# New order tables for VectorE, ScalarE, GpSimd and the transfer queue of a hybrid decoder layer

## The chip, the cores and the metric

The kernel runs on one core of a Trainium2 chip. A core has five instruction streams: TensorE (matmuls; PE in the rows, and PEld for its weight loads), VectorE (DVE), ScalarE (ACT), GpSimd (POOL) and SyncE (SP), which issues the transfers between memory and the core. Each engine works through its own instructions in the order in which they were written, and waits where an input is not there yet or a buffer is still in use. The metric is the time of one launch in microseconds on the device.

## The reference

One decoder layer on x of 512 positions by 1024 features, all in float32:

- h = RMSNorm(x), then one projection h @ w_in, whose columns are split among three groups of heads;
- gated DeltaNet, 4 heads of 128: a causal convolution of width 4 and SiLU on q, k and v, a decay and a beta per head from the gate columns, the delta rule in chunks of 64 (the inverse of a triangular matrix, then a state passed from chunk to chunk), a gated RMSNorm;
- S5, 32 groups of 16 channels: a diagonal complex state of 64 per group scanned over the positions, GELU, a gated linear unit (w_glu), RMSNorm;
- differential attention, 4 heads, two causal softmax maps per head subtracted with a learned factor, RMSNorm;
- x = x + concat(groups) @ w_out;
- x = x + (silu(gate) * up) @ w_down, where gate and up are a causal convolution of width 3 over RMSNorm(x) @ w_up (2 x 2816 columns); then a final RMSNorm.

The reference does these lines in this order:

```
g_q, g_k, g_v, g_z, g_b, g_a, s_u, d_q, d_k, d_v = split_cols(h @ w_in[i], IN_SIZES)
qkv = jax.nn.silu(causal_dwconv(jnp.concatenate([g_q, g_k, g_v], axis=-1), gdn_conv_w[i]))
x = x + jnp.concatenate([o_gdn, o_s5, o_diff], axis=-1) @ w_out[i]
x = x + conv_glu_ffn(rms_norm(x, ffn_norm_w[i]), ffn_w_up[i], ffn_conv_w[i], ffn_conv_b[i], ffn_w_down[i])
return rms_norm(x, final_norm_w)
```

## The kernel before

Every float32 product with a weight is done in three matmuls: the weight block (128 x 512, 256 KB, "wraw") is cast by ScalarE into a rounded high part ("whi", L566), VectorE subtracts it from the raw block for the low part ("wlo", L263), and TensorE adds high x high, low x high and high x low of weights and activations into one accumulator ("acc", helper at L182; transposes are the same instruction at L185). A block has three buffers, so its transfer (L564, on SyncE) starts when the block three before it has been used up. `wblock` (L555 to 568) does this for all weights.

The mixers take the first 465 us. Their generators run side by side: the projections (L1401 to 1426), the gates and decays of DeltaNet (gates L896 to 907 with the tile gg, decays L910 to 955), the convolutions `conv_silu` (L963 to 970: a product, three shifted multiply-adds into kq on VectorE, the sigmoid thc on ScalarE, a product), the DeltaNet chain (L1078 to 1225: scr and ms/rs are the norms of q and k, sc and lt the scaled triangular matrix, lct, xc, t_ and f_ the steps of its inverse), S5 (its scan L662, its outputs yu, which go out to memory and come back in another layout as yf: one write L694, four reads L696), and the differential heads (dv and dqk are copies of projections, L1252 and L1268; ka, kl, qa their split parts; pp the softmax). After that comes the output projection, and from 530 us the feed-forward network.

TensorE's order is a table of items (`ORDER`, L37), written out by hand and by a planner. When all is written, `in_order` (L135) pins the order of the four other engines: `SEQUENCE` (L55 to 129) has one list of numbers per engine, and the k-th number says which of the engine's instructions, counted as the program wrote them, stands at place k. SyncE's list is the order of the transfers in its queue; each issue there also waits for the landing of the one eight before it.

Of the kernel before, what the change touches and what calls it, by code (L numbers as in the profile page):

```python
# [78 lines left out]
784 779 787 782 790 785 794 788 774 791 777 793 780 783 800 786 789 792 801 795 802 1121-1122 796-799 1123 810 1124
803 1125-1126 804 806 811 815 805 807 816 808 1127-1128 812 821-822 813 809 814 817 826 818-819 827 823 832 820  # L80
824-825 833 828 837 829-830 838 831 834 843 835-836 844 839 848 840-841 849 842 845 854 846-847 855 850 859 851-852
860 853 856 865 857 867 858 869 861 866 871 862 868 873 863 870 875 872 874 877 879 864 876 881 878 882 880 886-887
883 892 884-885 893 888 897 889-890 898 891 894 903 895-896 904 899 908 900-901 909 902 905 914 906-907 915 910 919
911-912 920 913 916 925 917-918 927 921 929 922-923 926 931 924 928 933 930 935 932 937 934 939 936 941 938 942 940
946-947 943 952 944-945 953 948 957 949-950 958 951 954 963 955-956 964 959 968 960-961 969 962 965 974 966-967 975
970 979 971-972 980 973 976 985 977-978 987 981 989 982-983 986 991 984 988 993 990 995 992 997 994 999 996 1001 998
1002 1000 1006-1007 1003 1012 1004-1005 1013 1008 1017 1009-1010 1018 1011 1014 1023 1015-1016 1024 1019 1028
1020-1021 1029 1022 1025 1034 1026-1027 1035 1030 1039 1031-1032 1040 1033 1036 1045 1037-1038 1047 1041 1049
1042-1043 1046 1051 1044 1048 1053 1050 1055 1052 1057 1054 1059 1056 1061 1058 1062 1060 1066-1067 1063 1072
1064-1065 1073 1068 1077 1069-1070 1078 1071 1074 1083 1075-1076 1084 1079 1088 1080-1081 1089 1082 1085 1094  # L90
# [4 lines left out]
0-1 3 2 5 4 6-24 27 25 29 33 26 28 51 30 44 31 46 34-35 43 52 45 36 39 49 37 40 38 41-42 57 32 50 53 55-56 92 97
58-59 54 62-64 60 65-66 61 67 69-76 68 77-81 86-87 82-85 108 93-94 88-89 102-104 47 95 110 105-106 90 48 91 107 96
121 123 109 98 111-114 99-101 115-117 124-125 122 118 126 150-151 131-132 127-128 146 137-139 129 119 140 144 130
141 120 142 147 145 148-149 133-136 168 143 174 152-154 158 156 189 159 190-191 155 192 157 160-161 164 166 165 162
186 169 167 170-173 197-202 175 212 163 176 214 178 177 179 183 185 180 184 187 181 193-194 188 195-196 204-207 203
215 208-211 182 222-223 220 213 257 216 259 217 225 221 218 256 258 226 228 224 229 232 227 219 233 236 230 237 231  # L100
234 253 235 238-241 246-247 242-245 248-249 252 254 262 250-251 268 255 271 260-261 265 263-264 266-267 275 283 269
274 270 286 272-273 278-281 276-277 289 282 297-298 293-294 292 284 295-296 285 308 287-288 319 290-291 299-301 329
305 302 306 303 332 334 304 312 307 311 313 309-310 314 331 333 315-316 352 317 353 318 344 320 354-355 321-322 326
323 327 347 330 335 324-325 336-337 342 328 356-357 343 361 338-341 362-364 358 345 359 348 365-368 349 393 346 396
360 350-351 370-373 378 374-377 386 379 384-385 387 380-381 388 369 391 408 389-390 392 382 394-395 383 404 406 399
415 397-398 403 405 400-401 419 402 407 409-410 420 411-414 416 426 417 427 418 421-425 429 432 461-462 457-460 443
428 430-431 446 435 433-434 436-437 452 440-441 438-439 444-445 453 442 489 491 449 488 490 447 455 450 448 456 451
454 475 463 476 464-465 469 467 466 484 470 468 471 473 494 474 495-496 477 497 472 478-479 485 480-481 533 482-483
486-487 492 498 493 509-512 499-501 534 502 513-516 508 503 537 518-525 504-507 532 538 526-529 517 535 546 536
530-531 552 539-540 566 543-544 541-542 547-548 545 567 551 553-556 549-550 557-558 561 559-560 562-563 586-587  # L110
564-565 576 582-583 568 584 569 585 577 570-573 579 574-575 580-581 578 598 603 588-590 594 592 591 595 593 596-597
607 599-601 617 602 604-606 618 608-612 620 613-616 623 619 626 629 622 621 632 625 635 624 628 627 638 631 630 641
634 633 644 637 636 645 640 639 646 643 642 647 869-872 653 873 648 874-875 649 876 654 656 650 657 651 661 652 662
655 664 659 658 665 669 660 663 670 667 672 666 673 668 677 671 678 675 680 674 681 676 685 679 686 683 688 682 689
# [6 lines left out]
""",  # L121
    "gpsimd": """
0 4 1 10 3 5 7 6 57-60 9 8 11-12 61-62 13-19 21 26 20 22 27 30 33 36 39 28 31 34 37 40 29 32 35 38 41 45 42 46 43 47
44 48 66-67 23 50 25 49 54 51 53 52 56 55 68-69 63-65 70 73 75 72 74 71 78 80 77 79 76 81-83 85 87 86 84 88 90 92 89
91 94 93 95-130
""",
    "sync": """
# [1712 lines left out]
```

## Time and profile before

| | us |
|---|---|
| median of 3 runs | 829.7 (827.82 to 830.31) |
| the profiled execution | 831.47 |
| its span, first to last instruction | 829.3 |
| TensorE busy in the span | 792.8 |
| VectorE busy | 561.9 |
| ScalarE busy | 430.8 |
| GpSimd busy | 104.4 |

The mean granted clock of TensorE over the span is 0.972. The span is what the profiler saw of one execution; the 2.2 us between it and the execution's own time lie around the first and the last instruction. A share of busy time is a mean over stages: in the feed-forward part TensorE is busy all the time, in the mixers it waits here and there.

### The profile page before, as it was taken

Reading aid. Unit: us, or ns where it says so; the run is one execution under the profiler, and the core shown is the slowest. Engines: PE = TensorE matmul, PEld = TensorE weight load, DVE = VectorE, ACT = ScalarE, POOL = GpSimd, SP = SyncE. Lnnn points to the kernel's source line nnn. Section 1 sums busy time; section 2 is a strip of 40 time slices with the busy share of each in tenths; the row PEclk is TensorE's granted clock in tenths of the full one; section 3 lists DMA queues with packets and bytes.
Section 4 is the critical chain, followed back from the end, with each engine's and each line's share of the span. In section 5 each row is a group of like instructions: output and inputs, shape, how many; then the busy total and the mean of one; then the engine's idle time right before and its main releaser. Section 6 shows DMA issues by size and latency. Waiting matters only on the chain.

```text
span 829.3 us, 13695 instructions
## 1 busy us (share of the span) xinstructions
PE 792.8 (96%) x5004; PEld 653.9 (79%) x5004; DVE 561.9 (68%) x1159; ACT 430.8 (52%) x1001; POOL 104.4 (13%) x133
## 2 busy tenths in 40 slices
PE   6979989998999999999999999999999999999996
PEld 6868877986777878787777788788888888888885
DVE  8998898754757866548447976766557656657634
ACT  5266356644567966675547644344244334335423
POOL 5710000000001210010003211011001001001101
PEclk8998999998998999999989999999999999999998
DMA  6856453378383633341214532333333333333202
GB/s 158 102 94 51 92 77 87 61 111 61 81 45 53 44 67 72 94 70 55 84 44 125 182 100 83 107 102 90 101 90 101 102 89 102 95 96 100 78 1 102
DMA packets 133562, 71.58 MB, mean 86 GB/s; under 512 B 12766, under 2 KB 129784, under 8 KB 133496
## 3 DMA queue, kind: packets, MB, share of 16 engines
q1 hardware_dynamic: 133496, 70.72, 40.6%
q8 instruction: 39, 0.64, 0.3%
q14 instruction: 27, 0.22, 0.1%
HBM read 66.51 MB, written 4.19 MB: 85 GB/s over the span
## 4 chain that ended last, share of the span: by engine, by line
PE 74%; DVE 11%; DMA 6%; ACT 4%; issue 2%; POOL 1%; SPq 1%; POOLq 0%; DVEq 0%; ACTq 0%
PE acc L182 62%; PE gp L182 5%; PE sp L182 4%; DMA wraw<-in_w_in_dram 4%; DVE wlo L263 2%; DVE kq L269 1%; PE sp L185 1%; DVE z L263 1%; PE gp L185 1%; DMA yf<-swap 1%; ACT whi L566 1%; DVE ct L263 1%; DVE z L662 1%; ACT gm L1022 1%; DVE zt L263 0%
## 5 line engine op out<-in xcount | busy, mean ns | idle before, releaser
L566 ACT CAST whi<-wraw 128x512 fp32r<-128x512 f32 (+2 forms) x224 | 133.2, 597 | 169.1 <-PE acc L182 142.5
L182 PE MATMUL acc<-h,whi 128*128 128x512 f32 x704 | 217.7, 390 | 0.0
L263 DVE TENSOR_TENSOR wlo<-wraw,whi 128x512 fp32r<-128x512 f32 (+2 forms) x224 | 151.7, 680 | 55.7 <-ACT whi L566 49.9
L182 PE MATMUL acc<-hT,whi 128*128 128x512 f32 (+1 forms) x464 | 154.2, 409 | 4.7 <-ACT dv L1252 2.9
L182 PEld LDWEIGHTS acc<-h,whi 128*128 128x128 f32 x704 | 132.1, 188 | 28.6 <-DVE h L269 0.6
L182 PE MATMUL acc<-h,wlo 128*128 128x512 f32 x352 | 137.0, 390 | 0.0
L182 PEld LDWEIGHTS acc<-hT,whi 128*128 128x128 f32 x464 | 88.6, 198 | 20.6 <-ACT dv L1252 3.1
L182 PE MATMUL acc<-hT,wlo 128*128 128x512 f32 (+1 forms) x240 | 92.6, 398 | 0.0
L263 DVE TENSOR_TENSOR x<-x,acc 128x512 f32<-128x512 f32 (+1 forms) x65 | 44.0, 677 | 57.3 <-PE acc L182 57.3
L182 PEld LDWEIGHTS acc<-h,wlo 128*128 128x128 f32 x352 | 66.1, 188 | 14.0 <-DVE wlo L263 0.3
L269 DVE SCALAR_TENSOR_TENSOR ac<-us,rt,ac 128x511 f32<-128x511 f32 x88 | 65.9, 750 | 12.9 <-ACT ac L1719 11.5
L263 POOL TENSOR_TENSOR ac<-ac 128x512 f32<-128x512 f32 x22 | 35.6, 1619 | 280.5 <-DVE ac L269 161.3
L182 PE MATMUL acc<-ah,whi 128*128 128x512 f32 x144 | 57.6, 400 | 0.1
L182 PE MATMUL acc<-ah,wlo 128*128 128x512 f32 x144 | 56.5, 392 | 0.0
L182 PE MATMUL acc<-al,whi 128*128 128x512 f32 x144 | 56.0, 389 | 0.0
L401 POOL TENSOR_TENSOR rs<-ms,expo 128x4 f32<-128x4 f32 (+1 forms) x14 | 19.3, 1375 | 278.8 <-DVE ms L400 274.6
L182 PEld LDWEIGHTS acc<-hT,wlo 128*128 128x128 f32 x240 | 46.4, 198 | 7.5
L263 DVE TENSOR_TENSOR us<-acc,rb 128x512 f32<-128x512 f32 x44 | 30.3, 688 | 27.9 <-PE acc L182 27.9
L1719 ACT ACTIVATE ac<-us,rt 128x512 f32<-128x512 f32 x44 | 36.0, 817 | 21.5 <-DVE us L263 21.5
L263 DVE TENSOR_TENSOR al<-ac,ah 128x512 fp32r<-128x512 f32 x22 | 15.2, 691 | 28.1 <-ACT ah L1733 27.5
L182 PEld LDWEIGHTS acc<-ah,whi 128*128 128x128 f32 x144 | 27.1, 188 | 6.7 <-issue 1.1
L1733 ACT CAST ah<-ac 128x512 fp32r<-128x512 f32 x22 | 13.7, 622 | 35.8 <-POOL ac L263 35.8
(567 smaller groups left out, 1404.2 us busy)
## 6 DMA issues: line engine op xcount, KB each, us to landing
wraw<-in_ffn_w_up_dram SPq DMA_DIRECT2D x88, 256.0 KB
wraw<-in_w_in_dram SPq DMA_DIRECT2D x64, 256.0 KB
wraw<-in_ffn_w_down_dram SPq DMA_DIRECT2D x32, 256.0 KB
wraw<-in_w_out_dram SPq DMA_DIRECT2D x24, 128.0 KB
xt<-in_x_dram SPq DMA_DIRECT2D x4, 512.0 KB
xj<-in_x_dram SPq DMA_DIRECT2D x8, 256.0 KB
wraw<-in_w_out_dram SPq DMA_DIRECT2D x8, 256.0 KB
lwraw<-in_ffn_w_down_dram SPq DMA_DIRECT2D x8, 256.0 KB
```

Of the source, the lines that this page charges most:

```text
L182: pe(T.matmul(o, l, r, start=start, stop=stop))
L185: pe(T.transpose(o, i, ident_))
L263: e.tensor_tensor(o, a, b, op=op)
L269: e.scalar_tensor_tensor(o, a, s, b, op0=op0, op1=op1, **kw)
L401: ins = G.tensor_tensor(rs[:, :n], ms[:, :n], expo[:, :n], op=ALU.pow)
L566: S.copy(hi[:, :n], raw[:, :n])
L662: V.tensor_tensor_scan(zf[j], rr, zf[j], 0.0, ALU.mult, ALU.add)
L1022: S.activation(gm[:, n, :], m_ge, AF.Copy, scale=gp[:, n, h : h + 1])
L1719: S.activation(a, us, AF.Identity, scale=fcw(2, f), bias=fcb(f))
L1733: S.copy(ah[:, j, :], up)
```

## The change

Only the four lists of `SEQUENCE` differ: the lists for VectorE, ScalarE, GpSimd and SyncE are new. No instruction is added or taken away, TensorE's table is untouched, and the arithmetic is the same. Nearly all moves are in the first 465 us; a few lie between 463 and 530 us, and the last is a swap of two VectorE instructions at the very end. A list looks like this, so its numbers tell a reader nothing:

```diff
-98-102 114-117 107 118 108 119 109-111 120-123 128-195 200-219 223 348-351 224 352-355 225-347 356-363
+114-118 107 119-120 108-111 121-123 128-195 200-219 223 348-350 224 351-355 225-347 356-363
```

What it does is seen in the engines' orders, the old one with -, the new one with +.

First place: VectorE just ahead of the gate tile gg. gt is a chain of small steps towards it, z and zt are rotations of the S5 input, wlo is the low part of a weight block.

```order
 L263 TENSOR_TENSOR z<-sp,cs 128x512
 L269 SCALAR_TENSOR_TENSOR gt<-gt,gs 128x16
-L263 TENSOR_TENSOR cs<-cs,ct 128x512
+L263 TENSOR_TENSOR zt<-sp,cs 128x512
 L263 TENSOR_TENSOR gt<-gt,gmx 128x16
-L263 TENSOR_TENSOR z<-sp,cs 128x512
+L269 SCALAR_TENSOR_TENSOR zt<-sp,cs 128x512
 L269 SCALAR_TENSOR_TENSOR gg<-gt,al 128x16
-L263 TENSOR_TENSOR zt<-sp,cs 128x512
+L263 TENSOR_TENSOR wlo<-wraw,whi 128x512
 L944 CAST ghi<-gg 128x16
```

Both zt products now stand ahead of gg; a wlo that came after it has also moved ahead, further up than the piece shows.

Second place: ScalarE around the copy dv (the values of a differential head, out of the accumulator that TensorE fills next). ff are copies of the inverse's last step f__1437, d and enx parts of S5's tables.

```order
 L742 COPY wt<-sp 128x512 x2
-L1160 COPY ff<-f__1437 32x4x32
+L1160 COPY ff<-f__1437 32x4x32 x3
+L790 COPY enx<-en 64x32x16
 L773 COPY d_120<-sp 128x4x32
-L775 COPY d_120<-sp 32x4x32 x2
 L1252 COPY dv_1458<-acc 128x512
-L790 COPY enx<-en 64x32x16
-L775 COPY d_120<-sp 32x4x32
+L775 COPY d_120<-sp 32x4x32 x3
+L776 COPY d_120<-sp 64x4x32
```

Two more ff copies and an enx have moved ahead of dv, two d copies behind it.

Third place: VectorE and ScalarE where the second pair of heads has its keys and queries convolved (kq), about 190 to 210 us. VectorE before, from the first shifted step of the last kq on:

```order
L269 SCALAR_TENSOR_TENSOR kq<-acc,rt,kq 128x511
L269 SCALAR_TENSOR_TENSOR kq<-acc,rt,kq 128x510
L263 TENSOR_TENSOR wlo<-wraw,whi 128x512
L269 SCALAR_TENSOR_TENSOR kq<-acc,rt,kq 128x509
L269 SCALAR_TENSOR_TENSOR kq<-thc,kq 128x512
L400 TENSOR_SCALAR ms<-ss 128x8
L263 TENSOR_TENSOR wlo<-wraw,whi 128x512
L263 TENSOR_TENSOR sc<-rs,beta 128x4
```

And now:

```order
L269 SCALAR_TENSOR_TENSOR kq<-acc,rt,kq 128x511
L269 SCALAR_TENSOR_TENSOR kq<-acc,rt,kq 128x510
L269 SCALAR_TENSOR_TENSOR kq<-acc,rt,kq 128x509
L269 SCALAR_TENSOR_TENSOR kq<-thc,kq 128x512
L263 TENSOR_TENSOR wlo<-wraw,whi 128x512
L400 TENSOR_SCALAR ms<-ss 128x8
L263 TENSOR_TENSOR sc<-rs,beta 128x4
```

The wlo that stood between the second and the third step stands behind the whole kq, and the next wlo has moved from ahead of sc to behind lt. ScalarE in the same place, before (scr are the squares for the norms, kt the scaled keys):

```order
L963 ACTIVATE kq<-acc,rt 128x512
L566 CAST whi<-wraw 128x512
L968 ACTIVATE thc<-kq 128x512
L1078 ACTIVATE scr,ss<-gp 128x128 x4
L1081 ACTIVATE kt<-gp,ed 128x128 x2
L1078 ACTIVATE scr,ss<-gp 128x128 x4
L1081 ACTIVATE kt<-gp,ed 128x128 x2
L1268 ACTIVATE dqk<-acc 128x512
L566 CAST whi<-wraw 128x512 x2
L1115 COPY lct<-lt 32x128 x2
```

And now:

```order
L963 ACTIVATE kq<-acc,rt 128x512
L968 ACTIVATE thc<-kq 128x512
L566 CAST whi<-wraw 128x512
L1078 ACTIVATE scr,ss<-gp 128x128 x8
L1081 ACTIVATE kt<-gp,ed 128x128 x3
L1268 ACTIVATE dqk<-acc 128x512
L1081 ACTIVATE kt<-gp,ed 128x128
L1115 COPY lct<-lt 32x128
L566 CAST whi<-wraw 128x512
L1115 COPY lct<-lt 32x128
L566 CAST whi<-wraw 128x512
```

The cast of the same weight block has moved behind thc, and the cast of the block after it behind the first lct.

## Rows read from the trace of the kernel before

**Rows 1.** the page, part 1: busy us (share) xinstructions of each engine.
```profile
PE 792.8 (96%) x5004; PEld 653.9 (79%) x5004; DVE 561.9 (68%) x1159; ACT 430.8 (52%) x1001; POOL 104.4 (13%) x133
```

**Rows 2.** the chain that ended last: start us, us, what.
```profile
529.77 250.13 PE acc L182 x1098
```

**Rows 3.** timeline of TensorE: start us, us, what [idle before <- what ended it].
```profile
60.78 0.36 PE L182 MATMUL gp<-gg,m_ge 128*128 128x16 f32 x2 [3.36 <-DVE gg L269]
...
113.70 0.99 PE L182 MATMUL acc<-hT,whi 128*128 128x512 f32 x2 [2.94 <-ACT dv L1252]
...
138.62 0.60 PE L182 MATMUL sp<-cmx,wnx 128*128 128x32 f32 x4 [0.99 <-DVE yu L269]
...
200.67 1.12 PE L185 MATMUL gp<-ident,kq 128*128 128x128 f32 x4 [3.48 <-DVE kq L269]
...
208.28 0.61 PE L182 MATMUL acc<-hT,whi 128*128 128x512 f32 x2
...
292.17 0.45 PE L182 MATMUL gp<-t__3441,lct 32*32 32x32 f32 x32 [2.20 <-DVE t__3441 L263]
```

**Rows 4.** windows: us, busy PE PEld DVE ACT POOL, PEclk, DMA share, GB/s.
```profile
63.00:70.00 7.00, 6.56 (x24) 5.49 (x24) 6.87 (x18) 4.68 (x24) 0.00 (x0) 0.53 0.87 40
120.00:140.00 20.00, 18.30 (x145) 15.32 (x143) 19.71 (x39) 12.06 (x29) 0.00 (x0) 1.00 0.33 81
189.00:195.00 6.00, 6.00 (x28) 4.96 (x27) 4.65 (x7) 1.94 (x3) 0.00 (x0) 1.00 0.92 40
195.00:202.00 7.00, 3.52 (x21) 3.06 (x20) 2.04 (x3) 2.91 (x13) 0.00 (x0) 0.81 1.01 49
199.00:206.00 7.00, 5.33 (x15) 4.37 (x16) 1.03 (x3) 4.59 (x23) 1.64 (x1) 0.52 0.77 90
```

**Rows 5.** timeline of VectorE before the gate.
```profile
60.47 0.16 DVE L269 SCALAR_TENSOR_TENSOR gg<-gt,al 128x16 f32<-128x16 f32 x1
```

**Rows 6.** timeline of VectorE, 99 to 104.
```profile
102.80 0.69 DVE L263 TENSOR_TENSOR wlo<-wraw,whi 128x512 fp32r<-128x512 f32 x1 [2.62 <-ACT whi L566]
```

**Rows 7.** timeline of ScalarE, 111 to 114 and 199 to 200.
```profile
111.89 0.30 ACT L1160 COPY ff<-f__1437 32x128 f32<-32x128 f32 x1 [4.81 <-DVE f__1437 L1110]
...
113.54 0.62 ACT L790 COPY enx<-en 64x512 f32<-64x512 f32 x1
...
199.79 0.26 ACT L1078 ACTIVATE scr<-gp 128x128 f32<-128x128 f32 x1
```

**Rows 8.** the chain that ended last, 188 to 200.
```profile
188.13 9.01 DMA wraw<-in_w_in_dram
...
197.16 0.63 ACT whi L566
...
199.26 0.64 ACT thc L968
...
199.92 0.70 DVE kq L269
```

**Rows 9.** timeline of VectorE, 192 to 208.
```profile
192.99 1.53 DVE L269 SCALAR_TENSOR_TENSOR kq<-acc,rt,kq 128x511 f32<-128x511 f32 x2 [0.60 <-ACT kq L963]
...
203.05 0.17 DVE L400 TENSOR_SCALAR ms<-ss 128x8 f32<-128x8 f32 x1 [2.44 <-ACT scr L1078]
206.37 0.69 DVE L263 TENSOR_TENSOR wlo<-wraw,whi 128x512 fp32r<-128x512 f32 x1 [3.15 <-ACT whi L566]
...
207.60 1.13 DVE L269 SCALAR_TENSOR_TENSOR lt<-gp,sc,dec 128x128 f32<-128x128 f32 x4
```

**Rows 10.** timeline of GpSimd, 203.
```profile
203.37 1.64 POOL L401 TENSOR_TENSOR rs<-ms,expo 128x8 f32<-128x8 f32 x1 [32.06 <-DVE ms L400]
```

**Rows 11.** timeline of VectorE, 289 to 295.
```profile
289.21 1.23 DVE L1309 TENSOR_REDUCE dsm<-sp 128x2 f32<-128x1024 f32 x1
...
291.84 0.28 DVE L263 TENSOR_TENSOR t__3441<-ic,xc 128x128 f32<-128x128 f32 x1
...
294.27 0.75 DVE L269 SCALAR_TENSOR_TENSOR pp<-pp,dsm,pp 128x512 f32<-128x512 f32 x1
```

More of the change, by code (lines that the diff above doesn't have):

```diff
@@ new lines @@
+95-96 91 107 98 166 189 99 101 106 100 130 102 132 131 103 109 133 108 134-135 110 151 136 111-112 137-138 113 141
+114-115 142 116 155 139 117-118 143 119 140 147 144 152 126 148 220 145 167 146 149-150 156 127 153-154 168 157-158
+120 161 159-160 121 190-191 205 195 204 207-208 206 209 162 242 163-164 198-199 221 200 216 245 217 226 218 169 241
+170 244 171 243 219 172 246 173 201 174 222 175 202 176 223 177 254 178 224 179 203 180 272 181 225 182 228 183 227
+184 229 185 230 186 277 187 231 188 233 232 122 234 123-124 210 125 235 211 304 212-214 236 215 237 256 239 306 257
@@ new lines @@
+863 870 875 872 874 877 879 864 876 881 878 882 880 886-887 883 892 884-885 893 888 897 889-890 898 891 894 903
+895-896 904 899 908 900-901 909 902 905 914 906-907 915 910 919 911-912 920 913 916 925 917-918 927 921 929 922-923
+926 931 924 928 933 930 935 932 937 934 939 936 941 938 942 940 946-947 943 952 944-945 953 948 957 949-950 958 951
+954 963 955-956 964 959 968 960-961 969 962 965 974 966-967 975 970 979 971-972 980 973 976 985 977-978 987 981 989
+982-983 986 991 984 988 993 990 995 992 997 994 999 996 1001 998 1002 1000 1006-1007 1003 1012 1004-1005 1013 1008
@@ new lines @@
+1017 1009-1010 1018 1011 1014 1023 1015-1016 1024 1019 1028 1020-1021 1029 1022 1025 1034 1026-1027 1035 1030 1039
+1031-1032 1040 1033 1036 1045 1037-1038 1047 1041 1049 1042-1043 1046 1051 1044 1048 1053 1050 1055 1052 1057 1054
+1059 1056 1061 1058 1062 1060 1066-1067 1063 1072 1064-1065 1073 1068 1077 1069-1070 1078 1071 1074 1083 1075-1076
+1084 1079 1088 1080-1081 1089 1082 1085 1094 1086-1087 1095 1090 1099 1091-1092 1100 1093 1096 1105 1097-1098 1107
+1101 1109 1102-1103 1106 1111 1104 1108 1113 1110 1115 1112 1117 1114 1119 1116 1118 1120 1129-1147 1149 1148 1153
@@ L93 @@
+1150-1151 1155 1154 1152 1156-1158
 """,
     "scalar": """
[L95 to L98, printed above, removed]
@@ new lines @@
+333 315-316 352 317 353 318 344 354 320 355 321-322 326 323 327 347 335 330 324 336 325 342 337 356-357 343 361-362
+358-359 338-341 363 345 364 328 348-349 393 365-368 346 360 350-351 370-373 396 374-375 386 376-378 384-385 387
+379-381 388 369 391 389-390 392 408 382 394 383 395 404 406 399 403 405 397-398 400 415 401-402 419 407 409-410 420
+411-414 416 426 417 427 418 421-425 429 432 461-462 457-460 443 428 430-431 446 435 433-434 436 452 437 440-441
+438-439 444-445 453 442 489 491 449 488 490 447 455 450 448 456 451 454 475 463 476 464-465 469 467 466 484 470 468
@@ new lines @@
+471 473 494 474 495-496 477 497 472 478-479 485 480-481 533 482-483 486-487 492 498 493 509-512 499-501 534 502
+513-516 508 503 537 518-525 504-507 532 538 526-529 517 535 546 536 530-531 552 539-540 566 543-544 541-542 547-548
+545 567 551 553-556 549-550 557-558 561 559-560 562-563 586-587 564-565 576 582-583 568 584 569 585 577 570-573 579
+574-575 580-581 578 598 603 588-590 594 592 591 595 593 596-597 607 599-601 617 602 604-606 618 608-612 620 613-616
+623 619 626 629 622 621 632 625 635 624 628 627 638 631 630 641 634 633 644 637 636 645 640 639 646 643 642 647
@@ new lines @@
+869-871 653 872-875 648 876 654 649 656 650 657 651 661 655 652 662 659 664 658 665 660 669 663 670 667 672 666 673
+668 677 671 678 675 680 674 681 676 685 679 686 683 688 682 689 684 693 687 694 691 695 690 696-699 692 700-702
+704-705 709 703 710 707 712 706 713 708 717 711 718 715 720 714 721 716 725 719 726 723 728 722 729 724 733 727 734
+731 735 730 736 732 737-742 744-745 749 743 750 747 752 746 753 748 757 751 758 755 760 754 761 756 765 759 766 763
+768 762 769 764 773 767 774 771 775 770 776 772 777-782 784-785 789 783 790 787 792 786 793 788 797 791 798 795 800
@@ L125 @@
[L125 removed]
+0 4 1 10 3 5 7 6 57-60 9 8 11 61 12 62 13-19 21 26 20 22 27 30 33 36 39 28 31 34 37 40 29 32 35 38 41 45 42 46 43 47
+44 48 66-67 23 50 25 49 54 51 53 52 56 55 68 63 69 64-65 70 73 75 72 74 71 78 80 77 79 76 81-83 85 87 86 84 88 90 92
+89 91 94 93 95-130
 """,
     "sync": """
[L128 to L129 removed]
```

99 lines of the change are left out of this document (35 added, 64 removed).

## The prediction

> **What bounds the kernel now.** I read the page's busy times first: TensorE is busy 792.8 of 829.3 us, VectorE 561.9 [rows 1]. So all other work is hidden except 36.5 us in which TensorE stands. The chain that ended last says where that is not: from 529.77 on it is one unbroken run of 250.13 us of matmuls [rows 2]. The table moves almost nothing after 530 us, so the change is decided in the first 465 us, in the mixers. There I went through TensorE's own timeline for every row that has an idle time in front of it. The waits that the change can reach are the first 3.36 us for the gate tile gg at 60.78, 2.94 us for ScalarE's copy dv at 113.70, 0.99 us for yu at 138.62, 3.48 us for kq at 200.67 and 2.20 us for t_ at 292.17, 12.97 us together [rows 3]. Then the stretches by windows: after the waits for gg and kq the granted clock is 0.53 in 63 to 70 and 0.52 in 199 to 206 [rows 4], that is mostly the 1.2 GHz level, and the matmul row at 113.70 takes 0.99 us for two where the one at 208.28 takes 0.61 [rows 3]. A wait thus costs more than its own length. VectorE is the engine waited for in the first half: 19.71 of 20 us busy in 120 to 140 [rows 4].
>
> TensorE's order is the same but for one place near 470 us, where no idle row follows. So at each wait I ask only when the awaited tile comes in the new order, with the traced durations, against when TensorE arrives.
>
> **The gate, 60.78 (a loss).** gg was done at 60.63 [rows 5]. In the new order three 128x512 operations stand ahead of it that stood behind it, one wlo subtract and two zt, each 0.6 to 0.69 us (the wlo of 0.69 in [rows 6] is of that shape): +1.9 us. A cast of m_ltr and two table steps (0.6 us) join them, and the small dd product (0.6 us) leaves. Net +1.8 to +1.9; VectorE has no idle time ahead to absorb it. I take +1.8: the wait is 5.2 us instead of 3.4. What comes with it is the wlo and zt work done earlier, which is why the scans behind the gate can start sooner.
>
> **The copy dv, 113.70 (a gain).** ScalarE's dv stands behind a copy that waited 4.81 us for VectorE's transpose f__1437 [rows 7]. VectorE itself stood 2.62 us at 102.80, because the next in line was a wlo whose cast was not ready [rows 6]. The new order puts about 2.0 us of ready work (two products, a z add, t__1436) ahead of that wlo, which fills the hole, so f__1437 ends near 110.1 instead of 111.89. On ScalarE dv now has three ff copies of 0.30, one enx of 0.62 and one d copy of 0.27 ahead of it, 1.8 us, against ff and three d copies, 1.1 us: dv runs from about 111.9 to 112.5. TensorE, 1.8 late from the gate, wants it at 113.70 - 2.94 + 1.8 = 112.56. The wait goes, and TensorE stands at 112.6 where it stood at 113.70: -1.1. If TensorE does not stand there the clock may stay up, which is worth up to 1.7 (half of 3.4 us at half speed, from the 0.99 us pair); without the filled hole dv comes at 113.9 and the place costs +0.8 (two ff copies and enx less two d copies, and 0.2). I take -1.1.
>
> **yu, 138.62 (a gain).** VectorE is saturated up to it [rows 4], so yu comes as much earlier as the hole at 102.80 gave, 1.1 to 1.7. TensorE would need the same lead. I take a lead of -1.4 in total after this place (ends: +1.8, the gate's delay carried through, and -2.5).
>
> **kq, 200.67 (the largest term).** The last conv step of kq stood behind a wlo on VectorE that was the next in line, and the wlo waited for a weight block: issued at 188.13, 9.01 us on its way, then 0.63 us of cast [rows 8]. On ScalarE thc stood behind that cast too. In the new order both come behind kq. Then kq follows from its own chain: two steps end at 194.52 (192.99 and 1.53), a third takes about 0.75, thc 0.64, the product 0.70 [rows 8, 9], ready at 196.6. TensorE is free at 197.2 (200.67 - 3.48). No wait is left: -3.5, and if the clock stays up another 2.7 (5.3 us of matmuls at half speed).
>
> What is late next is the weights. After kq TensorE has 8 matmuls of the old block, then 12 of the block that landed at 197.14, all at 0.23 us: it wants the next block at 197.2 + 0.4 + 1.8 + 2.8 = 202.2. In the old run it took that block at 208.28 [rows 3]. The cast of that block stood ahead of the copies lct; it now stands behind the first, which needs lt from VectorE, which needs POOL's rs. Step by step: eight scr activations of 0.26 [rows 7] from 197.8 end near 199.8; ms 0.17, rs 1.64, the five sc steps 0.6, lt 1.13, lct 0.30 [rows 9, 10]: 203.9; cast 0.63: 204.5. The transfers give the same answer: of 256 KB a block, at 40 and 49 GB/s in 189 to 202 with the engines 0.92 to 1.01 busy [rows 4], the block after the one that landed at 197.14 lands 5.3 us later by estimate, 202.5, cast 203.1. So TensorE stands from 202.2 to 204.5, and again 0.3 for the wlo that follows. Net here 208.28 - 204.8 = -3.5; ends 0 (the clock falls after the new wait, which costs the same 2.7 to 3.4) and -6.1 (weights in time).
>
> On the transfers the Trainium skill (DMA: Bandwidth & Descriptors, its opening table of properties) has pieces of 512 B and more run at line rate. This trace disagrees: in 189 to 195 it shows 0.92 busy for 40 GB/s [rows 4]. By the page's rule the block would be there in time and the place would give the end of -6.1.
>
> **t_, 292.17 (small).** In the new order t__3441 comes ahead of a reduction and a kl. From that reduction's start to t__3441 are 2.6 us, of which the 0.4 of an xc stay ahead [rows 11]: 2.2 us earlier, so the 2.20 us go. But pp at 294.27 [rows 11] now stands behind two qa products, a dsm pair and a wlo; it ends near 296.2 instead of 295.0, while TensorE, early by 2, wants it at 294.2. The wait moves from t_ to pp, 2.0 of the 2.2 us come back. I take -0.3 (ends 0 and -2.2).
>
> **Nothing.** At the start the dd product and two queue swaps shift rows by under 1 us, covered by the first weight block. From 240 to 260 and around 465 to 475 single moves of 0.6 us stand beside TensorE at work with the next blocks already cast; if a block there is late it costs 0.6 each, +1.
>
> Sum: -1.4 - 3.5 - 0.3 = -5.2. The profiled run took 831.5 (span 829.3 and 2.2 around it), 1.8 above the median of 829.7; on it the sum gives 826.3, on the median 824.5. I say 824.7.
>
> **Rivals.** *Weights only (no change).* The wait for kq becomes a wait for the next block of the same size, since the transfers are full and the weight casts queue behind lct; the clock falls there as before. For: busy shares of 0.92 and 1.01. Against: the block needed at 202.2 was already under way. Then only the -1.4 and -0.3 stay: 828.0.
>
> *Full gain.* The waits at 113.70 and 200.67 go and the clock does not fall after them: -1.4 - 1.7 - 6.1 - 0.3 = -9.5, 820.2. For: both low stretches begin in these waits. Against: the block is not there at 202.2. The Trainium skill (TensorE: Matmul & The Clock Gate, The HAM clock gate) has the gate halve the clock after idleness, and full speed come back with work; the rows at 63 to 70 and 199 to 206 agree with 0.53 and 0.52 [rows 4]. By that rule, a shorter wait at 202 might not bring the clock down at all, and this case is the one that follows.
>
> *Slower: ScalarE starves TensorE of weights.* The new scalar order puts weight casts behind small copies that wait for VectorE at three places (around 205, 209 and 290). Price: the wait at 202 grows by the 2.5 us for which ScalarE idles ahead of lct, the low clock follows it (3.4), and the late pp at 294 keeps its 2.0: -1.4 - 3.5 + 2.5 + 3.4 + 2.0 = +3.0, 832.7. It decides from the point where the cast at 204.5 ends later than 208.28, the old time. Against: the chain scr to lct needs VectorE and POOL when both are nearly idle (2.44 us and 3.15 us waits there) [rows 9].
>
> **Numbers.** Forecast 0.45, full gain 0.17, weights only 0.20, slower 0.18. About 0.3% (2.5 us) is what a measurement can tell here: faster means under 827.2, slower over 832.2. The forecast's own range is 822 to 827, so faster is 0.45 + 0.17 = 0.62, same 0.20, slower 0.18. The range for 8 in 10 takes in the full gain and nearly reaches the slower case: 819.5 to 832.
>
> **What would show it.** Right: the row for gg with about 5 us of idle time, the wait for dv gone, the wait for kq gone, and a wait of some 2 us for whi three microseconds later; pp in place of t_ near 292. Wrong: kq still awaited; a wait for whi past 208; the clock at half through 204 to 211; or gg no later than now, which would mean that I misread what VectorE has to do ahead of it.

## The result, and the profile after

The changed kernel takes 819.64 us (median of 4 runs, 816.38 to 821.19) where the kernel before takes 829.07 (4 runs, 827.82 to 830.31): ratio 0.989, interval 0.9853 to 0.9927, or 9.4 us less. The forecast was 824.7. The direction was right. The range holds the time by a hair (it begins at 819.5). The number is close to the one worked out for the full gain (820.2), but not for that rival's reasons, as the section on the prediction shows.

The profiled run took 818.13 us (span 816.0), 1.5 below its median, and that of before 831.47, 2.4 above its own. So the two traces lie 13.3 us apart and the medians 9.4; what the other 3.9 are is told with the runs below.

Of the page, part 1 (busy us, share, instructions) and the first line of part 4 (shares of the chain that ended last), changed kernel:

```profile
PE 784.3 (96%) x5004; PEld 644.4 (79%) x5004; DVE 561.3 (69%) x1159; ACT 430.3 (53%) x1001; POOL 104.0 (13%) x133
PE 80%; DVE 10%; ACT 4%; issue 2%; DMA 2%; POOL 1%; POOLq 0%; DVEq 0%; ACTq 0%
```

The work is the same as in [rows 1], yet TensorE's busy time is 8.5 us shorter for the same 5004 matmuls: they ran at a higher clock. The other 4.8 us of the 13.3 are waits (36.5 us of the span before, 31.7 now). TensorE's timeline of the changed kernel (start, length, what, idle before), at the places of [rows 3]:

```profile
61.63 0.58 PE L182 MATMUL gp<-gg,m_ge 128*128 128x16 f32 x2 [5.59 <-DVE gg L269]
...
111.47 0.63 PE L182 MATMUL acc<-hT,whi 128*128 128x512 f32 x2
...
134.40 1.83 PE L182 MATMUL sp<-cmx,wnx 128*128 128x32 f32 x15 [0.72 <-DVE yu L269]
...
191.91 0.60 PE L185 MATMUL gp<-ident,kq 128*128 128x128 f32 x4
...
198.56 0.73 PE L182 MATMUL acc<-hT,whi 128*128 128x512 f32 x2 [1.46 <-ACT whi L566]
...
283.77 0.33 PE L182 MATMUL gp<-t__3610,lct 32*32 32x32 f32 x16 [1.21 <-issue]
...
454.06 0.73 PE L182 MATMUL acc<-h,whi 128*128 128x512 f32 x2 [0.93 <-DVE us L263]
```

The waits for dv, kq and t__3441 are gone; the one for gg has grown from 3.36 to 5.59; a wait for a weight cast (whi) stands 6.6 us behind kq, one of 1.21 near 284 and one of 0.93 at 454. TensorE stands at kq 8.76 us earlier than in [rows 3] (200.67 less 191.91), at the dv row 2.23 and at yu 4.22 earlier. Not all of this need belong to the change: the trace of before has a stretch of low clock at 18 to 22 us (0.57) that this one has not (1.00), and kernels with the same order there show both (see the table further down). Windows of the changed kernel (length, busy and count of PE, PEld, DVE, ACT, POOL, then granted clock, DMA share, GB/s):

```profile
63.00:70.00 7.00, 6.15 (x23) 5.09 (x23) 6.94 (x17) 5.19 (x25) 0.00 (x0) 0.50 1.00 43
112.00:120.00 8.00, 8.00 (x45) 6.92 (x44) 7.97 (x19) 5.70 (x13) 0.00 (x0) 1.00 0.49 74
160.00:240.00 80.00, 76.87 (x651) 62.03 (x650) 49.58 (x100) 44.62 (x113) 4.49 (x6) 1.00 0.70 79
195.00:202.00 7.00, 5.54 (x26) 4.03 (x25) 4.40 (x17) 2.24 (x7) 0.74 (x1) 1.00 0.55 96
240.00:300.00 60.00, 58.17 (x471) 46.51 (x469) 46.88 (x104) 48.66 (x144) 9.73 (x10) 1.00 0.44 56
```

and the same of before:

```profile
112.00:120.00 8.00, 6.30 (x23) 5.10 (x24) 7.05 (x16) 6.77 (x18) 0.00 (x0) 0.79 0.53 63
160.00:240.00 80.00, 76.25 (x624) 63.29 (x623) 48.56 (x98) 39.50 (x101) 2.85 (x3) 0.96 0.62 77
240.00:300.00 60.00, 55.74 (x415) 45.42 (x414) 46.46 (x100) 49.05 (x143) 9.87 (x12) 0.94 0.53 49
```

Behind the gate the clock falls to the 1.2 GHz level as before. Behind dv and behind kq it does not fall any more: 1.00 against 0.79 in 112 to 120 (0.21 of 8 us, 1.7 us of full-speed work) and 1.00 against 0.96 in 160 to 240. In 240 to 300 it was 0.94 before and 1.00 now, which is 3.6 us; whether that belongs to the change was the first question for the runs.

ScalarE's timeline of the changed kernel, where the new wait for whi comes from:

```profile
197.56 0.30 ACT L1115 COPY lct<-lt 32x128 f32<-32x128 f32 x1 [2.30 <-DVE lt L269]
197.88 0.62 ACT L566 CAST whi<-wraw 128x512 fp32r<-128x512 f32 x1
```

The cast at 197.88 stands behind a copy that waited 2.30 us for lt; it waited for nothing itself. This is the wait that the prediction put at 202.2 to 204.5.

### The profile page after: what moved, and what is told of

Same layout as the page of the kernel before. It is cut to its first block, busy times and chain, and to the rows that moved or that the text cites. A ratio compares the mean times of both kernels' runs of the same rounds, so it can differ in the third digit from the quotient of the medians.

```text
span 816.0 us, 13693 instructions
## 1 busy us (share of the span) xinstructions
PE 784.3 (96%) x5004; PEld 644.4 (79%) x5004; DVE 561.3 (69%) x1159; ACT 430.3 (53%) x1001; POOL 104.0 (13%) x133
## 4 chain that ended last, share of the span: by engine, by line
PE 80%; DVE 10%; ACT 4%; issue 2%; DMA 2%; POOL 1%; POOLq 0%; DVEq 0%; ACTq 0%
PE acc L182 67%; PE gp L182 5%; PE sp L182 5%; PE sp L185 2%; PE gp L185 1%; DVE wlo L263 1%; DMA wraw<-in_w_in_dram 1%; DVE z L263 1%; DMA wraw<-in_w_out_dram 1%; DVE kq L269 1%; PE acc L1607 0%; ACT gm L1022 0%; POOL rs L401 0%; DVE z L662 0%; ACT whi L566 0%
## 5 line engine op out<-in xcount | busy, mean ns | idle before, releaser
L182 PE MATMUL acc<-hT,whi 128*128 128x512 f32 (+1 forms) x464 | 148.9, 397 | 1.5 <-ACT whi L566 1.5
L182 PEld LDWEIGHTS acc<-hT,whi 128*128 128x128 f32 x464 | 84.9, 190 | 16.7 <-ACT whi L566 1.9
L182 PE MATMUL acc<-hT,wlo 128*128 128x512 f32 (+1 forms) x240 | 90.0, 386 | 0.1
L269 DVE SCALAR_TENSOR_TENSOR ac<-us,rt,ac 128x511 f32<-128x511 f32 (+1 forms) x88 | 65.8, 749 | 13.1 <-ACT ac L1719 11.7
L182 PEld LDWEIGHTS acc<-hT,wlo 128*128 128x128 f32 x240 | 44.6, 189 | 8.0 <-DVE wlo L263 0.7
```

Of the source, the lines that this page charges most:

```text
L182: pe(T.matmul(o, l, r, start=start, stop=stop))
L269: e.scalar_tensor_tensor(o, a, s, b, op0=op0, op1=op1, **kw)
```

## The experiments

Each ratio is against runs of the kernel before on the same chip, with its 95% interval; a gain in us is the ratio less 1, times the median of before there (828.58, 827.66 or 828.25). Diffs are rows of the order: - as before the edit, + as after it.

**The parts one by one.** Four kernels take the new order in one stretch each and the old one elsewhere: 0 to 40 us, 40 to 160, 160 to 230, and the rest. One row of each edit:

```diff
 start, DVE
+L411 TENSOR_SCALAR lr<-rt 128x16
 L1382 TENSOR_SCALAR ms_179<-ss_177 128x1
-L411 TENSOR_SCALAR lr<-rt 128x16
 gate and dv, ACT
 L623 ACTIVATE cmc<-sp 64x256
+L623 ACTIVATE cmx<-sp 64x16x16
 L726 COPY wnx<-wn 64x8x3x16
 kq, SP
-L564 DMA wraw<-in_w_in_dram 128x4x128 x4
+L564 DMA wraw<-in_w_in_dram 128x4x128 x5
 L694 DMA swap_2211<-yu 128x512
-L564 DMA wraw<-in_w_in_dram 128x4x128
 rest, DVE
+L263 TENSOR_TENSOR wlo<-wraw,whi 128x512
 L269 SCALAR_TENSOR_TENSOR pp_3543<-pp_3544,dsm,pp_3543 128x512
```

> Only the part of the new lists up to about 40 us; the rest as before. Theory of places (the gain is made where the order changed, and adds up): the two traces put the first matmul of the first weight block 0.7 us earlier and the low clock of 18.4 to 21.8 us gone, 1.5 us in all, so -1.5 (0 to -2). Rival (the start is no gain of its own, that stretch of low clock fell otherwise by chance): 0.

> Only the part of the new lists from about 40 to 160 us. Theory of places: the wait for gg grows by about 2, the wait for dv at 113.7 goes, yu comes earlier; the two traces have TensorE 3.5 us further ahead at 145 than at 24, so -3.5 (-2 to -4.5). Rival (my prediction's own term): -1.4. Rival two (the gain is made only together with the earlier start): +1.

> Only the part of the new lists from about 160 to 230 us. Theory of places: the wait of 3.5 for kq goes, the low clock of 199 to 206 with it (2.6), a wait of about 1.5 to 2 for the cast of the next weight block takes part of it back: -4.4 (-3.5 to -5). Rival (the clock falls after the new wait for weights as it fell after the one for kq): -1.5.

> Only the part of the new lists from about 230 us on. Theory of places: the wait for t at 292 goes and 1.6 of it come back, dg is 0.7 earlier, us 1.1 later: -0.5 (0 to -1.5); the stretches of low clock at 250 and 414, which the changed kernel does not have, stay or go here with no order of their own. Rival (these stretches were taken away by the later part of the lists): -5.

| part | median us | ratio | us by the ratio |
|---|---|---|---|
| start, 0 to 40 | 828.93 | 0.9998 [0.9972, 1.0024] | -0.2 |
| gate and dv, 40 to 160 | 824.92 | 0.9948 [0.9926, 0.997] | -4.3 |
| kq, 160 to 230 | 823.23 | 0.9941 [0.9915, 0.9967] | -4.9 |
| rest, from 230 | 828.17 | 1.0 [0.9968, 1.0031] | 0 |

The two middle parts add up to -9.2, and the whole gave -9.1 (0.011 of 829.07). The 1.5 us expected of the start did not come. The clock in 240 to 300 and the waits near 290 and 450 are not where the time came from: the rest alone gives nothing, and kernels that all have the old order there show a clock of 0.89 to 1.00 in 240 to 300. TensorE's timeline in the part for kq alone:

```profile
111.98 1.22 PE L182 MATMUL acc<-hT,whi 128*128 128x512 f32 x2 [2.52 <-ACT dv L1252]
...
201.42 0.73 PE L182 MATMUL acc<-hT,whi 128*128 128x512 f32 x2 [1.52 <-ACT whi L566]
...
283.53 0.45 PE L182 MATMUL gp<-t__3441,lct 32*32 32x32 f32 x32 [2.20 <-DVE t__3441 L263]
```

and in the part from 230 on alone:

```profile
201.27 1.12 PE L185 MATMUL gp<-ident,kq 128*128 128x128 f32 x4 [3.79 <-DVE kq L269]
...
293.62 0.63 PE L185 MATMUL sp<-ident,pp 128*128 128x128 f32 x4 [1.08 <-DVE pp L269]
```

Each part removes its own wait and leaves the others much as they were in [rows 3]. In the last one the 2.20 us for t__3441 become 1.08 for pp, as predicted.

**Only 40 to 230 new.** The edits of the two middle parts together.

> Only the two parts from 40 to 230 us new. If the gain is made there and adds up: -9.2, as the whole change. Rival (the start's and the end's moves carry something that single runs could not tell): 1 to 2 us less than the whole.

820.82 us, 0.9917 [0.9884, 0.995]: -6.9, with ends of -9.6 and -4.1, where -9.2 was expected. The changed kernel, run again on the same chip:

> The changed kernel once more, for a closer interval beside the others: the parts alone gave 0, -4.3, -4.9 and 0 us, so -9.2 if they add up (ratio 0.989). Rival (the first 4 runs were lucky in the clock): -6.

821.19 us (819.25 to 824.13, 6 runs), 0.9919 [0.9889, 0.9949], or -6.7 with ends of -9.2 and -4.2: smaller than the -9.1 of the first comparison, within both intervals. The two middle parts (-6.9) hold the whole of it. Here too the whi wait stands (1.45 us at 197.38) and the one near 284 (1.56 at 282.89).

**Two moves for kq.** The kernel before with only the wlo and the cast put behind kq.

```diff
 DVE
-L263 TENSOR_TENSOR wlo<-wraw,whi 128x512
 L269 SCALAR_TENSOR_TENSOR kq<-acc,rt,kq 128x509
 L269 SCALAR_TENSOR_TENSOR kq<-thc,kq 128x512
+L263 TENSOR_TENSOR wlo<-wraw,whi 128x512
 ACT
-L566 CAST whi<-wraw 128x512
 L968 ACTIVATE thc<-kq 128x512
+L566 CAST whi<-wraw 128x512
```

> The kernel before with two moves only: on VectorE the wlo ahead of the last step of kq goes behind kq, on ScalarE the cast of the same block goes behind thc. Theory (these two are the whole third part): -4.5 to -5.5, the wait for kq gone, TensorE's next wait at the following weight block, which is cast as in the kernel before. Rival (the other moves of that part, loads and casts in another order, carry half of it): -2.5.

826.27 us, 0.9984 [0.9965, 1.0003]: -1.3, which the interval doesn't tell from nothing, and not the 4.5 to 5.5 of the theory. That these two moves are the third part's gain fell with it. TensorE's timeline of this kernel:

```profile
202.66 0.73 PE L182 MATMUL acc<-hT,whi 128*128 128x512 f32 x2 [1.41 <-ACT whi L566]
...
208.72 0.45 PE L182 MATMUL gp<-t__2484,lct 32*32 32x32 f32 x32 [1.64 <-DVE t__2484 L263]
```

ScalarE's, the casts with a wait:

```profile
201.99 0.62 ACT L566 CAST whi<-wraw 128x512 fp32r<-128x512 f32 x1 [1.45 <-DMA wraw<-in_w_in_dram]
...
204.97 0.62 ACT L566 CAST whi<-wraw 128x512 fp32r<-128x512 f32 x1 [2.36 <-DMA wraw<-in_w_in_dram]
```

and the weight load of [rows 8] in this kernel, from the chain that ended last:

```profile
187.26 9.05 DMA wraw<-in_w_in_dram
```

kq is no longer awaited, but 3.05 of its 3.48 us come back, and now the casts wait for transfers. The blocks come as late as before: this load lands 0.83 us earlier than in [rows 8], and TensorE is 0.95 us further ahead here anyhow (195.18 at the row `gp<-kq` ahead of kq, 196.13 before). What the moves do save is the low clock: it is 1.00 in 202 to 210, behind the new wait.

TensorE's order is the same in all these kernels, so the place can be timed by itself: from that row `gp<-kq` to the matmul that stands at 220.07 in the kernel before. It takes 23.94 us there and 23.03 to 24.10 in the four other kernels with the old order here (mean of the five 23.51), and 21.38 in this one. So the trace has 2.1 us at the place where the runs have -1.3 in all.

Why the blocks come late, the chain that ended last shows in the kernel before, ahead of the load that [rows 8] begin with (start, length, what):

```profile
180.25 5.73 DMA yf<-swap
...
186.15 0.64 ACT yh L812
...
186.81 0.06 DVE yl L269
...
187.42 0.69 DVE wlo L263
188.13 9.01 DMA wraw<-in_w_in_dram
```

The load at 188.13 could not be issued until its buffer was free. What frees it is a wlo that stood on VectorE behind yl, and yl waits for the cast yh of the state read back through memory (yf). A chain that has nothing to do with kq sets when kq's weights start.

**The queue alone.** The kernel before with the other half of the third part: weight loads ahead of the swap write and the yf reads, yl and yh behind the wlo's and casts; the order around kq stays.

```diff
 SP
 L696 DMA yf<-swap_1960 32x4x128 x4
-L564 DMA wraw<-in_w_in_dram 128x4x128 x4
+L564 DMA wraw<-in_w_in_dram 128x4x128 x5
 L694 DMA swap_2211<-yu 128x512
-L564 DMA wraw<-in_w_in_dram 128x4x128
-L696 DMA yf<-swap_2211 32x4x128
-L564 DMA wraw<-in_w_in_dram 128x4x128
-L696 DMA yf<-swap_2211 32x4x128 x3
+L564 DMA wraw<-in_w_in_dram 128x4x128 x2
+L696 DMA yf<-swap_2211 32x4x128 x4
 DVE
+L269 SCALAR_TENSOR_TENSOR kq<-acc,rt,kq 128x511
 L269 SCALAR_TENSOR_TENSOR yl<-yf,yh 128x512
-L263 TENSOR_TENSOR wlo<-wraw,whi 128x512 x2
-L269 SCALAR_TENSOR_TENSOR kq<-acc,rt,kq 128x511
```

> The kernel before with the third part's moves up to 192 us alone: the weight loads ahead of the swap's write and reads, yh and yl behind, kq's wlo and cast where they were. Theory (the old chain of waits was yf, yh, yl, a wlo queued behind yl, the buffer that it frees, and only then the weight load that kq's wlo waited for): the load that was issued at 188.1 goes out some 3 us earlier, the wait for kq falls from 3.5 to about 0.5, -2.5 to -4. Rival (kq's place in the order is what counts): the wait stays 3 or more, 0 to -1.

825.58 us, 0.9968 [0.9946, 0.9991]: -2.7. The chain that ended last, of this kernel:

```profile
183.88 0.70 DVE wlo L263
...
184.60 10.19 DMA wraw<-in_w_in_dram
...
196.16 0.67 DVE kq L269
...
198.32 1.11 PE gp L185 x4
```

The load is issued 3.53 us earlier than in [rows 8], without yl in the chain, though it then takes 10.19 us instead of 9.01; it lands 2.35 earlier and TensorE stands 2.35 earlier at kq (200.67 less 198.32). Of this, 0.89 is TensorE's lead ahead of the place (195.24 at `gp<-kq`); against the kernel with the two moves, which is as far ahead, the load goes out 2.66 earlier (187.26 less 184.60). The wait left is 2.02 us where 0.5 was expected, since the transfer itself took longer and TensorE comes earlier. The two halves give -1.3 and -2.7, together -4.0; with the intervals this can be the -4.9 of the part, and a bonus for doing both is not shown. The place by itself takes 21.51 us here, 2.0 less than the mean of 23.51, and 19.33 to 19.43, or 4.1 less, in the four kernels with both halves (kq alone, 40 to 230, changed, changed again). In the traces the halves are equal and add up.

**The hole not filled.** The part for gate and dv with six VectorE instructions around the hole at 102.80 in the old order.

```diff
 DVE
+L263 TENSOR_TENSOR z<-z,zt 128x512
+L263 TENSOR_TENSOR wlo<-wraw,whi 128x512
 L263 TENSOR_TENSOR ct<-fa,gb 128x512
-L263 TENSOR_TENSOR z<-z,zt 128x512 x2
 L263 TENSOR_TENSOR t__1436<-t__1381,gp 128x128
 L263 TENSOR_TENSOR cs<-cs,ct 128x512
-L263 TENSOR_TENSOR wlo<-wraw,whi 128x512
+L263 TENSOR_TENSOR z<-z,zt 128x512
```

> The part from 40 to 160 us alone, but with the six VectorE instructions around the hole at 102.8 in the old order. Theory (filling that hole brings f__1437 and so dv forward): the hole of about 2.5 us is back, f__1437 and dv come 1.5 to 2 later, a wait for dv of 1 to 2 us is back, and of the -4.3 of that part about -2.5 stays. Rival (the casts and loads in their new order bring the wlo itself earlier, so there is no hole to fill): -4.3, no wait for dv.

826.22 us, 0.9968 [0.9945, 0.9992]: -2.7, against -4.3 with the hole filled. VectorE's timeline without the fill:

```profile
100.70 0.69 DVE L263 TENSOR_TENSOR wlo<-wraw,whi 128x512 fp32r<-128x512 f32 x1 [1.80 <-ACT whi L566]
...
109.47 0.30 DVE L1110 STREAM_TRANSPOSE f__1437<-t__1436 128x128 f32<-128x128 f32 x1
```

with it (the part for gate and dv):

```profile
107.44 0.30 DVE L1110 STREAM_TRANSPOSE f__1437<-t__1436 128x128 f32<-128x128 f32 x1
```

and in the part for kq alone, which has the old order up to 160 us:

```profile
101.08 0.69 DVE L263 TENSOR_TENSOR wlo<-wraw,whi 128x512 fp32r<-128x512 f32 x1 [2.21 <-ACT whi L566]
...
109.83 0.30 DVE L1110 STREAM_TRANSPOSE f__1437<-t__1436 128x128 f32<-128x128 f32 x1
```

The fill brings f__1437 2.03 us earlier, as worked out from the prediction's 2.0. Without it f__1437 is 2.08 earlier than the 111.55 of before, but only 0.36 earlier than in the part for kq alone, whose clock in 18 to 22 is 1.00 as here (0.57 before); the kernel with the same start is the fair one to compare with. TensorE at dv without the fill:

```profile
112.06 0.73 PE L182 MATMUL acc<-hT,whi 128*128 128x512 f32 x2 [0.76 <-ACT dv L1252]
```

In the part for kq alone it stands there at 111.98, after 2.52 us. So without the fill dv comes no earlier. TensorE comes 1.84 us later, after the longer wait at the gate and the low clock behind it, waits only 0.76, and the clock stays at 1.00 in 112 to 120 (0.80 in kq alone, 1.6 us). With the fill dv is not awaited and TensorE stands there at 110.78. The fill is thus worth some 1.3 us in the traces and 1.6 in the runs (-4.3 less -2.7; the intervals, 0.9945 to 0.9992 and 0.9926 to 0.997, overlap); what the part gains without it is, by these traces, the clock.

**The gate's delay taken back.** The changed kernel with the two zt and one wlo behind gg.

```diff
 DVE
+L263 TENSOR_TENSOR gt<-gt,gmx 128x16
+L269 SCALAR_TENSOR_TENSOR gg<-gt,al 128x16
 L263 TENSOR_TENSOR zt<-sp,cs 128x512
-L263 TENSOR_TENSOR gt<-gt,gmx 128x16
+L263 TENSOR_TENSOR wlo<-wraw,whi 128x512
```

> The changed kernel with gg brought forward: both zt and the wlo go behind gg again, as they stood before. Theory (my sum: the gate's delay is a loss): gg 1.8 earlier, the wait for it 3.8 in place of 5.6; TensorE then comes 1.8 earlier to dv, which ends only 0.3 before it is wanted, so a wait for dv of 1.5 comes back and -0.3 is left. Rival (TensorE alone sets the time between the two places): -1.8.

822.74 us, 0.9919 [0.989, 0.9949]: nothing gained (the changed kernel has 0.989 and 0.9919). TensorE's timeline:

```profile
59.90 0.37 PE L182 MATMUL gp<-gg,m_ge 128*128 128x16 f32 x2 [2.69 <-DVE gg L269]
...
62.40 0.79 PE L182 MATMUL gp<-gm,m_ltr 128*128 128x512 f32 x1 [1.39 <-ACT gm L1022]
64.28 0.79 PE L182 MATMUL gp<-gm,m_ltr 128*128 128x512 f32 x1 [1.09 <-ACT gm L1022]
```

gg comes 1.73 us earlier (61.63 less 59.90), as expected, and the wait for it falls by 2.90, since TensorE comes later to it. But TensorE then waits for gm, 2.48 us in two rows where the changed kernel has 0.84, and the second gm row is only 0.42 earlier (64.70 less 64.28). The time did come back, but not as a wait for dv: dv is not awaited, and TensorE is there at 111.31 (changed 111.47). It came back at once, behind gg. This trace also has a clock of 0.79 in 198 to 206, behind a whi wait of 1.55 us, where the changed kernel has 1.00; those 1.7 us are not the gate's.

**The cast ahead of lct.** The changed kernel with the cast of 197.88 put ahead of the last kt and the copies lct.

```diff
 ACT
 L1268 ACTIVATE dqk<-acc 128x512
+L566 CAST whi<-wraw 128x512
 L1081 ACTIVATE kt<-gp,ed 128x128
-L1115 COPY lct<-lt 32x128
-L566 CAST whi<-wraw 128x512
-L1115 COPY lct<-lt 32x128
+L1115 COPY lct<-lt 32x128 x2
```

> The changed kernel with one move: the cast of the weight block that TensorE awaited for 1.46 us at 198.6 goes ahead of the copies lct on ScalarE. Theory (the wait is ScalarE's queue; the block landed 1.5 us before its cast began): the wait falls to 0.1 for the cast and up to 0.7 for the wlo behind it, -0.8. Rival (the transfers set it): 0.

818.0 us (814.91 to 823.01), 0.9885 [0.9848, 0.9921]. The wait of 1.46 is gone; 0.63 for the wlo behind it is left. ScalarE's cast:

```profile
194.67 0.62 ACT L566 CAST whi<-wraw 128x512 fp32r<-128x512 f32 x1 [0.93 <-DMA wraw<-in_w_in_dram]
```

It now starts as the block lands, 3.21 us before the 197.88 of the changed kernel, of which 1.27 is TensorE's lead (189.75 against 191.02 at `gp<-kq`). So the block had been there for some 1.9 us, by estimate, and the wait was ScalarE's order. The place takes 18.29 us instead of 19.33. In the median the step is within what can be told.

**A better version.** The changed kernel with three awaited instructions put ahead of ones that need nothing of them: the cast as above, pp ahead of a wlo at 282, and the steps rb and us ahead of low-part casts at 453.

```diff
 DVE
-L263 TENSOR_TENSOR wlo<-wraw,whi 128x512
 L269 SCALAR_TENSOR_TENSOR pp_3543<-pp_3544,dsm,pp_3543 128x512
+L263 TENSOR_TENSOR wlo<-wraw,whi 128x512
-L263 TENSOR_TENSOR lwlo<-lwraw,lwhi 128x512 x5
+L263 TENSOR_TENSOR lwlo<-lwraw,lwhi 128x512 x2
 L263 TENSOR_TENSOR us<-acc,rb 128x512
```

> The changed kernel with three waits mended: the weight cast at 198 ahead of lct (as in the run before), pp ahead of the wlo at 282, rb and us ahead of the last low parts of the down weights at 453. Theory: 1.5, 0.6 and 1.0 us of waits go, -2 to -3 against the changed kernel. Rival (each wait moves to the next tile, as at 292): 0 to -1.

817.91 us (814.96 to 820.42, 6 runs), 0.9881 [0.985, 0.9912], where the changed kernel on the same chip has 821.19: 3.3 us less. TensorE's waits near the three places:

```profile
196.58 0.50 PE L182 MATMUL acc<-hT,wlo 128*128 128x512 f32 x1 [0.63 <-DVE wlo L263]
...
280.75 0.63 PE L185 MATMUL sp<-ident,pp 128*128 128x128 f32 x4 [0.53 <-DVE pp L269]
```

Of 1.46, 1.21 and 0.93 there are 0.63, 0.53 and 0 left. It beats the kernel before; against the changed kernel its six runs overlap in one microsecond (819.25 to 820.42), and against the cast alone (0.9885) the intervals tell nothing apart.

## Why the prediction was right or wrong

**Right.** The order of events: kq no longer awaited, a wait for whi in its place (1.46 us, predicted 2.3), gg with 5.59 (predicted 5.2), dv not awaited, t__3441's wait turned into one at pp, and nothing from the start and the rest. TensorE came for the late block 5.19 us after kq (197.10 less 191.91), as in the sum (5.0); the "three microseconds later" among the signs does not fit that sum. The 5.59 is in part luck: of the 2.23 by which that wait grew, 0.85 is gg coming later and the rest TensorE coming earlier. The rival in which the wait only changes its name is what the two moves for kq alone do (3.05 of 3.48 us come back), but for the clock, which that rival had fall and which stayed at 1.00.

**Wrong, first: the second part, -1.4, measured -4.3.** The trace to compare with is not that of before but that of the part for kq alone: same order up to 160 us, and the clock in 18 to 22 is 1.00 in it as in the part for gate and dv. In the trace of before it is 0.57, and VectorE, with the same order up to there, is 1.01 us later at 43 us (the tile pl at 43.58, and at 42.57 in kq alone). TensorE's timeline, kq alone:

```profile
60.36 0.43 PE L182 MATMUL gp<-gg,m_ge 128*128 128x16 f32 x2 [2.33 <-DVE gg L269]
...
63.42 0.79 PE L182 MATMUL gp<-gm,m_ltr 128*128 128x512 f32 x1 [0.37 <-ACT gm L1022]
```

and the part for gate and dv:

```profile
61.52 0.58 PE L182 MATMUL gp<-gg,m_ge 128*128 128x16 f32 x2 [5.60 <-DVE gg L269]
...
64.60 0.80 PE L182 MATMUL gp<-gm,m_ltr 128*128 128x512 f32 x1 [0.37 <-ACT gm L1022]
...
110.78 0.63 PE L182 MATMUL acc<-hT,whi 128*128 128x512 f32 x2
```

- "Net +1.8 to +1.9" at the gate came out smaller: gg comes 1.16 later (at most 1.7, if the 0.54 us that VectorE stands ahead of gg in kq alone are left out), the second gm 1.18, and TensorE is at dv's place 1.32 later (110.78; 109.46, which is 111.98 less 2.52). That the delay is carried there was right. The three operations ahead of gg are worth 1.73 at gg and 0.42 at the second gm, by the run above, so other moves have a share in it, which was not tested.
- "I take -1.1" at dv was right for the place itself: 111.98 to 110.78, -1.2. f__1437 ended at 107.74, earlier than the predicted 110.1.
- The step that failed is what comes behind: the clock, "worth up to 1.7", was left to a rival and put at nothing in the sum, and the lead after the place was taken as -1.4. The clock in 112 to 120 is 1.00 against 0.80, 1.6 us, and at the row `gp<-kq` ahead of kq the lead is 4.0 (193.81 less 189.81), near the measured -4.3. The -1.2 and the 1.6 make 2.8; the other 1.2 lies behind 120, where the clock in 122 to 150 is 1.00 against 0.94 (1.7 us). By the table that clock falls in kernels of either order, so whether this piece belongs to the change is open.

In the 14 profiles the granted clock in 112 to 120 goes with the wait for dv without exception: 0.57 to 0.80 in the six kernels that wait for dv 2.51 to 3.03 us, 1.00 in the eight that wait 0.76 or not at all.

The table gives it beside three other windows; the last lies behind all that the middle parts move:

| kernel | clock 18 to 22 | 112 to 120 | 122 to 150 | 396 to 420 |
|---|---|---|---|---|
| before | 0.57 | 0.79 | 0.94 | 0.88 |
| start alone | 1.00 | 0.58 | 1.00 | 1.00 |
| kq alone | 1.00 | 0.80 | 0.94 | 0.86 |
| rest alone | 0.50 | 0.57 | 1.00 | 1.00 |
| two moves for kq | 0.64 | 0.79 | 0.94 | 0.86 |
| the queue alone | 0.65 | 0.79 | 0.94 | 0.86 |
| gate and dv alone | 1.00 | 1.00 | 1.00 | 1.00 |
| the hole not filled | 1.00 | 1.00 | 0.94 | 0.86 |
| 40 to 230 | 1.00 | 1.00 | 0.94 | 0.86 |
| changed | 1.00 | 1.00 | 1.00 | 1.00 |
| changed, again | 1.00 | 1.00 | 1.00 | 0.86 |
| the gate's delay taken back | 1.00 | 1.00 | 1.00 | 1.00 |
| the cast ahead of lct | 1.00 | 1.00 | 1.00 | 0.86 |
| the better version | 1.00 | 1.00 | 1.00 | 0.86 |

The column for 112 to 120 follows the order. That for 396 to 420 does not: one and the same kernel shows 1.00 and 0.86. Nor does that for 18 to 22: kernels with the old order up to 40 us show 0.50 to 1.00. The traces of before and of the changed kernel differ by 1.7 us in 18 to 22 (0.43 of 4 us) and by 2.9 in 396 to 420 (0.12 of 24), more than the 3.9 by which they lie further apart than the medians. Two profiles of kernels that are equal in a stretch can thus lie 3 us apart, and 34 runs of the kernel before spread from 823 to 833.

**Wrong, second: the third part, -3.5, measured -4.9.** The size is within the interval of [-7.0, -2.7] that 0.9915 to 0.9967 gives; the mechanism is half wrong. The step "the block needed at 202.2 was already under way" looked at when blocks land and not at what frees their buffers. The prediction's -3.5 came from the two moves alone, and these gave -1.3 (2.1 at the place in the trace). The rest came from the queue: loads issued 2.7 us earlier since yl and yh no longer stand in front of the wlo that frees the buffer (-2.7; 2.0 at the place). The swap and yl moves were in the diff; they were given no value. A slip in the working is small: the steps to lct add up to 203.6, not 203.9. And the sum adds this term to the lead although it was worked out at the old times, with no lead; that the two add was not argued, but within the intervals the runs bear it out (-9.2 in parts, -6.9 and -9.1 together).

**The full gain.** The clock stayed up behind the 1.46 us wait (1.00 in 195 to 202), as that rival said, and behind the 5.59 us at the gate it fell (0.50 in 63 to 70). The rule of the Trainium skill that was set beside it (TensorE: Matmul & The Clock Gate, The HAM clock gate) agrees with both. The clock is not sure to stay up: of six profiles with a whi wait of 1.41 to 1.55 us there, five show 1.00 and one 0.79. The chance of 0.17 was too low because the prediction asked for weights in time, when a shorter wait was mostly enough. That 820.2 nearly came out is luck: its terms were -1.4, -1.7, -6.1 and -0.3, and the parts gave -4.3, -4.9 and nothing.

## What to carry to other kernels

When an instruction waits for a transfer, ask what let the transfer be issued: follow the chain back to the instruction that frees its buffer, and to what stands in front of that one. Price work that is put ahead of an awaited tile by the whole path behind it, not by that tile: here three operations moved gg by 1.73 us and the tile after it by 0.42, and the delay that was left ran into a place where TensorE had stood 2.5 us anyhow. Count the low-clock stretch behind a wait as part of the wait's price, but take small terms from several timed runs of each part, since one profile can differ from the next by more than the term. Before two traces are laid side by side at one place, see that their clocks agree ahead of it; a kernel that differs from the other only there is the one to compare with.

## What the runs showed of the hardware that was not expected

In the changed kernel, too, the weight loads are slow in one stretch. The transfers of the changed kernel, 180 to 200 (40 slices: busy tenths, GB/s):

```profile
DMA  5899999989999789989999999999998986522220
GB/s 120 83 97 75 88 103 175 72 45 38 35 35 40 19 37 33 48 38 38 37 34 35 35 44 39 51 60 50 87 159 144 211 178 101 95 34 27 38 62 4
```

In slices 9 to 28 the engines are 0.7 to 0.9 busy and move 19 to 60 GB/s; in 29 to 33 they are 0.8 or 0.9 busy and move 87 to 211. The loads have the same shape in both (256 KB, pieces under 2 KB). What the engines do in the slow slices is open; it was not tried.

The same wait at the same place can leave the clock up or bring it down. Eight kernels wait 2.19 or 2.20 us for t__3441, between 279 and 293 us. In 8 us from there on the granted clock is 1.00 in five of them and 0.79 in three. The window of before, and that of the start alone, in both behind 2.20 us:

```profile
292.00:300.00 8.00, 7.83 (x133) 6.46 (x134) 5.61 (x15) 4.91 (x13) 0.00 (x0) 1.00 0.18 53
292.00:300.00 8.00, 7.48 (x122) 6.04 (x123) 5.88 (x15) 4.50 (x12) 0.00 (x0) 0.79 0.15 42
```

The length of a wait alone does not say whether the clock falls.
